# A two-layer encoder on one core: head and attention ordered as one graph by a list scheduler, with negated logits and the sink as a column of the logits

## The chip, the core and the metric

The kernel runs on one core of one Trainium2 chip. The metric is device time in microseconds: from the start to the end of one execution. TensorE (PE) multiplies matrices into PSUM, VectorE (DVE) and ScalarE (ACT) work on tiles in SBUF and PSUM, GpSimd (POOL) is nearly unused, SyncE (SP) and ScalarE issue DMAs. Each engine takes its instructions in the order of the program, and waits on semaphores for the others.

## The reference

Two request groups (512 and 256 tokens, 1024 features) pass through two layers with shared weights. Layer 0 mixes tokens by windowed attention, layer 1 by a short convolution; each is followed by an MLP and by a gated input embedding.

```python
def trunk(x, p, rel_bias, ...):
    band_bias, in_window = band_geometry(rel_bias)
    for i in range(DEPTH):                                  # DEPTH = 2
        h = rms_norm(x, norm_mix[i])
        if i % N_MIXERS == 0:
            x = x + window_attention(h, attn_w_qkv[j], attn_w_o[j], attn_sink[j], band_bias, in_window)
        else:
            x = x + short_conv(h, conv_w_in[j], conv_w[j], conv_w_out[j])
        h = rms_norm(x, norm_mlp[i])
        x = x + jnp.square(jax.nn.relu(h @ mlp_w_up[i])) @ mlp_w_down[i]
        gate = jax.nn.sigmoid(rms_norm(x, norm_ple[i]) @ ple_w_gate[i])
        x = x + (p[i] @ ple_w_proj[i]) * gate
    return rms_norm(x, final_norm)

# in window_attention, for each block of 128 queries (a block sees itself and its two neighbours):
logits = einsum(q, k) * scale + band_bias
logits = jnp.where(valid, logits, NEG_INF)
m = jnp.maximum(jnp.max(logits, axis=-1, keepdims=True), sink_logit)
pexp = jnp.exp(logits - m)
denom = jnp.sum(pexp, axis=-1, keepdims=True) + jnp.exp(sink_logit - m)
probs = pexp / denom                                        # then probs @ v, and @ w_o
```

There are 16 query heads and 4 key heads of 64 features; four query heads share a key head. All is fp32.

## The kernel before

Activations lie transposed, features on the 128 partitions and the 768 tokens of both groups in the free dimension. An fp32 product is made of three fp32r matmuls: each operand is split into a high part (a ScalarE copy) and a low part (VectorE subtracts the high part from the source), and high by high, high by low and low by high are added up in PSUM (`split`, `weight`, `group`). A product over 768 tokens is a matmul of 512 and one of 256 columns, three times for each of the eight blocks of features.

`mixer_attention` is the stage that the change rewrites. It comes first in the program; the MLPs, the gated embeddings and the convolution follow, and their code stays.

The head of the stage stands in the order that is written, on ScalarE, TensorE, VectorE and SyncE (`manual_schedule`). It loads the first input embedding `p`, its projection, `x` in eight blocks and the first weights; projects the embedding (`step`, stored to `pj` in DRAM); scales and splits `x` (`Norm.block`, tiles `xs_mix`), sums its squares, makes the row of relative-position biases (`bp`, `brow`) and the first keys' product.

Behind it nothing fixes the order by hand: the framework orders the instructions from where they stand in the code and from buffers and dependencies. There the row of biases is stored 32 times, shifted, to DRAM (`skew`); the reciprocal norms follow (`rstd`), keys (`keys`: two chunks of two key heads, copied to both halves of the partitions by DMA, tiles `khh` and `kll`), queries (`queries`: eight chunks of two heads, copied by DMA to tiles `q`) and values (`values`, tiles `vp` in PSUM and `vv`).

`attend(g)` then runs for the four key heads over six blocks of 128 tokens (four of the first group, two of the second). A block has two or three key blocks, so its scores are 256 or 384 columns wide. For each block:

- scores of four heads, two matmuls each, into PSUM tiles `S` (L690, L691);
- `tensor_tensor_reduce` on VectorE (L692) adds the bias, writes logits to `L` (two heads to a tile, five buffers) and takes the maximum with the sink to `mx`;
- `nm` negates the maximum (L705), `es` is the exponential of the sink less the maximum (L707, L708);
- ScalarE takes exponentials in place with a running sum `sm` (L712); `es` is added (L713) and the sum inverted (L714);
- each head's row is scaled, the first of four on ScalarE (`NA = 1`, L718), three on VectorE (L720);
- for each key block TensorE transposes four heads to `pt` (L725), ScalarE copies to `ph` (L733), VectorE makes the low part `pl` (L734), and two matmuls add to `O` (L735, L736; one PSUM bank);
- ScalarE copies the lower half of `O` to `ot` (L738), VectorE adds the halves into `heads` (L743).

`beside` hands queries, the second keys, part of the second embedding's projection and the first output projections to fixed blocks, behind which their code stands. `load_bias` reads shifted windows of `skew`: for key heads 0 and 1 through ScalarE's queue, for 2 and 3 through SyncE's. Output projections (`output_part`, tiles `aos`, `w_o0`, `w_o1`) add to `xa`; the last of them run after the stage, in matmuls of 384 columns (L128).

Of the kernel before, what the change touches and what calls it, by code (L numbers as in the profile page):

```python
# [31 lines left out]
NA = 1  # L32
# [14 lines left out]
def trunk_kernel(ctx: ExitStack, tc: tile.TileContext, a: dict, out: bass.AP):  # L47
# [10 lines left out]
    act.preload_act_table_set(EXP_LN)  # L58
# [10 lines left out]
    sink = const.tile([P, HEADS], F32, name="sink")  # L69
    ident = const.tile([P, P], F32, name="ident")  # L70
# [393 lines left out]

    def mixer_attention():
        s1, s2 = ExitStack(), ExitStack()
        psum = s2.enter_context(tc.tile_pool(name="psK", bufs=3, space=PSUM))
        nonlocal tmp
        ap = s1.enter_context(tc.tile_pool(name="attn", bufs=2))
# [6 lines left out]
        def pair(j, name, dt=F32):  # L476
            return main.tile([P, 2, T], dt, tag=f"x{j}", name=name)

        x = [pair(j, "x_in") for j in range(KB // 2)]

        def xin(m):
            return x[m // 2][:, m % 2, :]

        ET = mybir.EngineType
        order = {ET.Activation, ET.PE, ET.DVE, ET.SP}
        norm = Norm(0, "mix0", range(16, 32), 0)
        xs = norm.xs

        split_products = False

        def products(terms):

            if not split_products:
                ps = psum.tile([P, 1024], F32, tag="mm", name="mm")
                group(ps, terms)
                yield ps[:, :T], 0, T
                return
            o = 0
            for i, n in enumerate(SEQS):
                ps = psum.tile([P, 512], F32, tag=f"mm{i}", name="mm", bufs=BM)  # L500
                group(ps, [(wh, wl, xh[:, o : o + n], xl[:, o : o + n]) for wh, wl, xh, xl in terms], n)
                yield ps[:, :n], o, o + n
                o += n

        def step(l, m, w, part, tag, vector):

            if tag == "L":
                t = ap.tile([P, T], F32, tag="L", name="pjs", bufs=BL)
            else:
                t = big("pjs")  # L510
            for ps, o, e in products(terms_of(w, part, col=m % 4 * P)):
                if vector:
                    dve.tensor_copy(t[:, o:e], ps)
                else:
                    act.activation(t[:, o:e], ps, AF.Copy)
            nc.sync.dma_start(pj[l][m], t[:])

        with tc.manual_schedule(engines=order):
            w0 = wp.tile([P, CH], F32, name="wraw", bufs=3)
            p0 = []  # L520
            for k in range(2):
                c = slice(512 * k, 512 * k + 512)
                nc.sync.dma_start(w0[:, c], a["proj"][0, 0, :, c])
                t = big("p")
                nc.sync.dma_start(t[:], a["p"][0, :, k, :])
                p0.append(t)
            w1 = fetch(a["proj"][0, 1])
            nc.sync.dma_start(vec[:], a["vec"][:])
            for m in range(KB):
                nc.sync.dma_start(xin(m), a["x"][m])  # L530
            wk = fetch(a["w_k"][0])
            rb = ap.tile([32, HEADS], F32, name="rb", bufs=1)
            nc.sync.dma_start(rb[:], a["rel_bias"][:])
            oh = ap.tile([32, 512], F32, tag="bias", name="oh", bufs=4)
            nc.sync.dma_start(oh[:], a["onehot"][:])
            mk = ap.tile([HEADS, 512], F32, tag="bias", name="mk", bufs=4)
            nc.sync.dma_start(mk[:], a["mask"][:].broadcast_to([HEADS, 512]))
            nc.sync.dma_start(sink[:], a["sink"][:].broadcast_to([P, HEADS]))

            hi = wp.tile([P, CH], F32R, name="whi", bufs=2)  # L540
            lo = wp.tile([P, CH], F32R, name="wlo", bufs=2)
            part0 = [], []
            for k in range(2):
                c = slice(512 * k, 512 * k + 512)
                split(hi[:, c], lo[:, c], w0[:, c])
                ph, pl = slot(10 + k, "p0h"), slot(12 + k, "p0l")
                split(ph[:], pl[:], p0[k][:])
                part0[0].append(ph[:])
                part0[1].append(pl[:])
            w0 = blocks(hi[:], 2), blocks(lo[:], 2)  # L550
            w1 = weight(None, 2, raw=w1)
            for i in range(KB):
                step(0, i, (w0, w1)[i // 4], part0, "L", i % 2)
                norm.block(i, xin(i))
                if i == 3:
                    wk = weight(None, KB, raw=wk)
                    wq = [fetch(a["w_q"][0])]

            bp = psum.tile([P, 512], F32, tag="S", name="bp", bufs=2)
            pe.matmul(bp[:HEADS, :], lhsT=rb[:], rhs=oh[:], start=True, stop=True)  # L560
            brow = tmp.tile([HEADS, 512], F32, tag="t", name="brow")
            dve.tensor_tensor(brow[:], bp[:HEADS, :], mk[:], ALU.add)
            kps = list(products(terms_of(wk, xs)))
            wq[0] = weight(None, KB, raw=wq[0])
            ss = norm.sum_squares(psum)

        with s1:
            rawv = [fetch(a["w_v"][:, :T])]
            wq.append(fetch(a["w_q"][1]))

            skew = dram.tile([HEADS, (ROWS + 1) * SKEW], F32, name="skew")
            nc.sync.dma_start(
                skew[:, : ROWS * SKEW].rearrange("h (i m) -> h i m", i=ROWS),
                brow[:, None, :SKEW].broadcast_to([HEADS, ROWS, SKEW]),
            )
            rawv += [fetch(a["w_v"][:, o : min(o + T, 2 * CH)]) for o in (T, 2 * T)]
            r = norm.rstd(psum, ss=ss)


            def keys(c, kps):  # L580
                t = big("kt")
                for ps, o, e in kps:
                    dve.tensor_tensor(t[:, o:e], ps, r[:, o:e], ALU.mult)
                hi = big("kh", F32R)
                lo = big("kl", F32R)
                split(hi[:], lo[:], t[:])
                for j in range(2):
                    g = 2 * c + j
                    khh[g], kll[g] = slot(KHI[g], "khh"), slot(KLO[g], "kll")
                    for dst, part in ((khh[g], hi), (kll[g], lo)):  # L590
                        for i in range(2):
                            nc.sync.dma_start(
                                dst[64 * i : 64 * i + 64, :].bitcast(F32),
                                part[64 * j : 64 * j + 64, :].bitcast(F32),
                            )

            def queries(c):
                w = wq[0] if c == 0 else weight(a["w_q"][c], KB, raw=wq[1] if c == 1 else None)
                t = big("qt")
                for ps, o, e in products(terms_of(w, xs)):  # L600
                    dve.scalar_tensor_tensor(t[:, o:e], ps, HD**-0.5, r[:, o:e], ALU.mult, ALU.mult)
                hi = big("qh", F32R)
                lo = big("ql", F32R)
                split(hi[:], lo[:], t[:])
                for j in range(2):
                    h = 2 * c + j
                    qst[h] = slot(QS[h % 8], "q")
                    for i, part in enumerate((hi, lo)):
                        nc.sync.dma_start(
                            qst[h][64 * i : 64 * i + 64, :].bitcast(F32),  # L610
                            part[64 * j : 64 * j + 64, :].bitcast(F32),
                        )

            rc = ap.tile([P, T // P], F32, name="rc", bufs=1)
            rt = psum.tile([P, 512], F32, tag="S", name="rt", bufs=2)
            for n in range(T // P):
                pe.transpose(rt[:, n : n + 1], r[0:1, n * P : (n + 1) * P], ident[0:1, 0:1])
            dve.tensor_copy(rc[:], rt[:, : T // P])
            keys(0, kps)


            vv = ap.tile([P, T // P, KV, 2, HD], F32R, name="vv", bufs=1)
            wv = [], []
            for i, raw in enumerate(rawv):

                m = min(T, 2 * CH - i * T)
                hi, lo = slot((4, 8, 10)[i], "wvh"), slot((5, 9, 11)[i], "wvl")
                split(hi[:, :m], lo[:, :m], raw[:, :m])
                for parts, t in zip(wv, (hi, lo)):
                    parts += blocks(t[:, :m], m // 256)  # L630
# [14 lines left out]
            for i in range(2):  # L645
                queries(i)
# [991 lines left out]
```

## Time and profile before

| | before |
|---|---|
| median of 3 runs | 1666.8 us (1666.33 to 1667.81) |
| profiled execution, span from first to last instruction | 1665.8 us |
| mean granted TensorE clock over the span | 0.994 |
| busy: TensorE, VectorE, ScalarE | 1637.0, 1407.8, 912.1 us |
| DMA, mean over the span | 87 GB/s |
| first matmul | 5.81 us |
| first matmul of the stage behind attention | 276.99 us |

A profile row names the line of the code, the engine and operation, the tiles as output<-inputs, the shape and how often it ran; then the busy time and the mean duration of one in ns, and the idle time just before such instructions with what ended it. PEld are TensorE's weight loads, which overlap its matmuls. A busy TensorE may still be slow, since matmuls overlap: the distance from start to start says how fast it really goes.

### The profile page before, as it was taken

What the parts mean: (1) busy time and instruction counts of PE and PEld (TensorE: products, weight loads), DVE (VectorE), ACT (ScalarE), POOL (GpSimd) and SP (SyncE); (2) the same over time, 40 slices, a digit from 0 to 9 for tenths busy, and PEclk for the clock granted to TensorE, in tenths of its full rate; (3) what the DMA queues carried; (4) which work ended last, traced back from release to release, by engine and by line L of the source; (5) the groups of instructions that cost most, each with busy time, mean ns of one, the idle gap of its engine ahead of it and who ended that gap; (6) DMA issues with size and microseconds to landing.
All of it is one profiled execution on the core that took longest, in us unless ns stands there. A gap on an engine that the chain in (4) does not pass through costs nothing. (4 is left out here: it accounts for less than half of the span.)

```text
span 1665.8 us, 24155 instructions
## 1 busy us (share of the span) xinstructions
PE 1637.0 (98%) x9422; PEld 1587.7 (95%) x9422; DVE 1407.8 (85%) x2305; ACT 912.1 (55%) x1448; POOL 1.0 (0%) x12
## 2 busy tenths in 40 slices
PE   8999999999999999999999999999999999999996
PEld 7888878999999999999999999999999999999986
DVE  6489888999899889977878887759989989998776
ACT  6377756855555555544654434555545545554555
POOL 0000000000000000000000000000000000000000
PEclk9999999999999999999999999999999999999998
DMA  8735422212222222232321222211222222222222
GB/s 265 180 113 145 136 76 73 99 57 70 76 77 69 72 76 66 74 96 73 114 67 58 77 66 78 82 54 51 76 64 86 67 72 70 75 76 79 80 86 99
DMA packets 47843, 144.59 MB, mean 87 GB/s; under 512 B 6080, under 2 KB 10688, under 8 KB 47728
## 3 DMA queue, kind: packets, MB, share of 16 engines
q1 hardware_dynamic: 46448, 141.47, 26.8%
q10 hardware_dynamic: 1280, 1.57, 0.4%
q8 instruction: 74, 1.21, 0.3%
q14 instruction: 41, 0.34, 0.1%
HBM read 123.10 MB, written 10.48 MB: 80 GB/s over the span
## 5 line engine op out<-in xcount | busy, mean ns | idle before, releaser
L428 ACT ACTIVATE whi<-sum 128x1024 fp32r<-128x1024 f32 x66 | 70.1, 1062 | 257.1 <-PE a L460 214.4
L460 PE MATMUL a<-xs,whi 128*128 128x384 f32 x608 | 118.1, 335 | 0.7 <-DVE y L1135 0.7
L460 PEld LDWEIGHTS a<-xs,whi 128*128 128x128 f32 x608 | 106.5, 188 | 1.6 <-DVE y L1135 1.3
L460 PE MATMUL b<-t,zhi 128*128 128x384 f32 x528 | 107.4, 336 | 0.0
L460 PE MATMUL a<-t,whi 128*128 128x384 f32 x528 | 107.3, 336 | 0.0
L460 PE MATMUL a<-t,zhi 128*128 128x384 f32 x528 | 107.2, 336 | 0.0
L1171 DVE TENSOR_TENSOR x<-x,a 128x384 f32<-128x384 f32 x112 | 62.1, 554 | 53.1 <-PE a L460 53.0
L460 PE MATMUL a<-act,whi 128*128 128x384 f32 x448 | 95.8, 334 | 0.0
L460 PEld LDWEIGHTS a<-t,zhi 128*128 128x128 f32 x528 | 93.3, 188 | 0.0
L460 PEld LDWEIGHTS b<-t,zhi 128*128 128x128 f32 x528 | 93.2, 188 | 0.0
L460 PEld LDWEIGHTS a<-t,whi 128*128 128x128 f32 x528 | 93.2, 188 | 0.0
L428 ACT ACTIVATE zhi<-sum 128x1024 fp32r<-128x1024 f32 x66 | 69.8, 1057 | 37.2 <-DVE sum L404 31.4
L439 DVE TENSOR_TENSOR wlo<-wraw,whi 128x1024 fp32r<-128x1024 f32 x72 | 87.7, 1217 | 0.0
L428 ACT ACTIVATE whi<-wraw 128x1024 fp32r<-128x1024 f32 x72 | 75.6, 1050 | 19.3 <-issue 15.8
L137 PE MATMUL mm<-xs_mix,whi 128*128 128x512 f32 (+1 forms) x320 | 82.9, 344 | 0.0
L439 DVE TENSOR_TENSOR zlo<-sum,zhi 128x1024 fp32r<-128x1024 f32 x66 | 80.3, 1217 | 0.5 <-ACT zhi L428 0.5
L439 DVE TENSOR_TENSOR wlo<-sum,whi 128x1024 fp32r<-128x1024 f32 x66 | 80.4, 1218 | 0.0
L460 PEld LDWEIGHTS a<-act,whi 128*128 128x128 f32 x448 | 79.3, 188 | 0.0
L82 ACT ACTIVATE whi<-wraw 128x1024 fp32r<-128x1024 f32 (+2 forms) x49 | 49.9, 1020 | 39.2 <-PE mm L128 15.0
L460 PE MATMUL a<-xs,wlo 128*128 128x384 f32 x304 | 65.0, 334 | 0.0
L83 DVE TENSOR_TENSOR wlo<-wraw,whi 128x1024 fp32r<-128x1024 f32 (+2 forms) x49 | 57.6, 1176 | 5.7 <-ACT whi L82 5.7
L460 PE MATMUL b<-t,zlo 128*128 128x384 f32 x264 | 61.1, 336 | 0.8 <-DVE zlo L439 0.8
(286 smaller groups left out, 4491.5 us busy)
## 6 DMA issues: line engine op xcount, KB each, us to landing
wraw<-in_up SPq DMA_DIRECT2D x64, 512.0 KB, 3.4
wraw<-in_down SPq DMA_DIRECT2D x64, 512.0 KB, 3.4
wraw<-in_w_in SPq DMA_DIRECT2D x24, 512.0 KB, 3.4
wraw<-in_gate SPq DMA_DIRECT2D x16, 512.0 KB, 3.4
pj<-pjs SPq DMA_DIRECT2D x16, 384.0 KB, 2.8
wraw<-in_w_q SPq DMA_DIRECT2D x8, 512.0 KB, 4.5
wraw<-in_w_out SPq DMA_DIRECT2D x8, 512.0 KB, 3.5
x_in<-in_x SPq DMA_DIRECT2D x8, 384.0 KB, 7.1
```

The source lines that it names most:

```text
L82: first = act.activation(hi, src, AF.Copy)
L83: dve.tensor_tensor(lo, src, hi.bitcast(F32), ALU.subtract)
L137: pe.matmul(ps[:, o:e], lhsT=w, rhs=x[:, o:e], start=i == 0 and j == 0, stop=i == n - 1 and j == 2,)
L428: act.activation(hi[:], src, AF.Copy)
L439: dve.tensor_tensor(lo[:], src, hi[:].bitcast(F32), ALU.subtract)
L460: pe.matmul(ps, lhsT=a, rhs=b, start=start and i == 0, stop=i == len(terms) - 1, skip_group_check=True)
L1171: dve.tensor_tensor(t[:, o : o + H], t[:, o : o + H], f, op)
```

## The change

Everything in `mixer_attention` becomes an operation of a graph (`Plan.op`) with an engine, a cost from a small formula, what it runs `after`, and which buffers it uses. A buffer's next use waits for all users of the one before (`Plan.ring`). `Plan.order` walks over the engines in modelled time, takes on each the ready operation with the longest way to the end (operations of attention on TensorE get a bonus of 10 us), and the code is emitted in that order, with `manual_schedule` on all five engines. The product of two blocks is an operation for each block of features (three matmuls), so products of several PSUM tiles can alternate.

In the computation: queries are scaled by the negative of the old factor and the bias row is negated, so `S` and `L` hold negated logits and the reduce takes a minimum with the negated sink (`nsink`); the exponential runs with scale -1 and that minimum as its bias. Column 0 of each head in `L` holds the negated sink, copied there by POOL; the exponential runs over it too, so the sum holds the sink's share, and `nm`, `es`, its exponential and the addition go. `NA` becomes 2. All bias loads go through SyncE. At the start, six matmuls of ones run before the first product, with the bias row between them; its inputs come through ScalarE's queue, and the load of the activation table stands behind those.

```diff
-NA = 1
+NA = 2
+URGENT = 10.0
...
+    class Plan:
+        OWN = {"PE": 0.0, "ACT": 0.13, "DVE": 0.12, "POOL": 0.1, "SP": 0.0}
+        OTHER = {"PE": 0.22, "ACT": 0.15, "DVE": 0.14, "POOL": 0.3, "SP": 0.1}
...
+        def order(self):
...
+            for o in reversed(self.ops):
+                tail = o.tail if o.tail is not None else self.OTHER[o.engine]
+                o.reach = o.cost + max((n.reach + (tail if o in n.after else 0.0) for n in nexts[id(o)]), default=0.0)
...
+            while any(waiting.values()):
+                best = None
+                for e, os in waiting.items():
+                    if os:
+                        t = max(free[e], min(o.ready for o in os))
+                        o = max((o for o in os if o.ready <= t), key=lambda o: o.reach + o.bonus)
+                        if best is None or t < best[0]:
+                            best = t, o
+                t, o = best
+                waiting[o.engine].remove(o)
+                o.start = t
+                free[o.engine] = t + o.cost
+                if o.tail is not None:
+                    pipe = max(pipe, t + o.cost + 1.7) + o.tail
+                    o.landed = pipe + 0.3
...
+        def A(n):
+            return 0.095 + 0.00084 * n
+        def V(n):
+            return 0.067 + 0.00104 * n
+        MM = {512: 0.2275, 256: 0.12}
...
+        rb_in = dma(rb, lambda: (rb.t[:], a["rel_bias"][:]), 2048, queue="ACT")
+        oh_in = dma(oh, lambda: (oh.t[:], a["onehot"][:]), 65536, queue="ACT")
+        mk_in = dma(mk, lambda: (mk.t[:], a["mask"][:].broadcast_to([HEADS, 512])), 32768, queue="ACT")
+        table = op("ACT", 1.28, lambda: act.preload_act_table_set(EXP_LN), behind=[mk_in])
...
+        d0 = first(warm, "PE", 3 * 0.45, dummy(3), [wide], [ones512.key])
+        bps = first(bp, "PE", 1.0, ..., [rb_in, oh_in, d0], [rb.key, oh.key])
+            lambda: dve.scalar_tensor_tensor(brow.t[:HEADS, :512], bp.t[:HEADS, :], -1.0, mk.t[:], ALU.mult, ALU.subtract),
+        d1 = op("PE", 3 * 0.3, dummy(3), [bps], [warm.key, ones512.key])
...
-                                dve.tensor_tensor_reduce(
-                                    L[:, j, :w],
-                                    S[:, :w],
-                                    bias[hp][:, j, j0 : j0 + w],
-                                    1.0,
-                                    sink[:, h : h + 1],
-                                    ALU.add,
-                                    ALU.max,
-                                    accum_out=mx[:, 2 * hp + j : 2 * hp + j + 1],
-                                )
...
-                        dve.tensor_scalar(nm[:], mx[:], -1.0, None, ALU.mult)
-                        dve.tensor_tensor(es[:], sink[:, hs], mx[:], ALU.subtract)
-                        act.activation(es[:], es[:], AF.Exp)
...
-                            act.activation(Lh, Lh, AF.Exp, bias=nm[:, h : h + 1], accum_out=sm[:, h : h + 1])
-                        dve.tensor_tensor(sm[:], sm[:], es[:], ALU.add)
...
+                    sunk = first(L, "POOL", 0.2, lambda L=L, H_=H_: nc.gpsimd.tensor_copy(
+                        L.t[:, :, 0:1], nsink[:, H_ : H_ + 2].rearrange("p (a b) -> p a b", b=1)), [turned])
...
+                    dve.tensor_tensor_reduce(
+                        L.t[:, j, 1 : 1 + w], S.t[:, :w], bias[hp].t[:, j, j0 : j0 + w], 1.0,
+                        nsink[:, H_ : H_ + 1], ALU.add, ALU.min, accum_out=mn.t[:, h : h + 1],
+                    )
+                args = "DVE", 0.40 if nk == 2 else 0.53, reduced, [s, bias[hp].ready, sunk, turned]
...
+                    act.activation(L.t[:, j, : 1 + w], L.t[:, j, : 1 + w], AF.Exp, bias=mn.t[:, h : h + 1], scale=-1.0,
+                                   accum_out=sm.t[:, h : h + 1])
...
+                args = "DVE", V(256), joined, [o_, last]
...
+        load_bias(0)
+        unit(2, "n")
+        unit(3, "t")
+        group_of_heads(0)
+        load_bias(1)
+        second_keys()
+        second_projected()
...
+            with tc.manual_schedule(engines={ET.Activation, ET.PE, ET.DVE, ET.SP, ET.Pool}):
+                for o in plan.order():
+                    o.run()
```

More of the change, by code (lines that the diff above doesn't have):

```diff
@@ L489, in mixer_attention @@
[L489 to L513, printed above, removed]
-                else:
[L515 to L520, printed above, removed]
-            for k in range(2):
[L522 to L565, printed above, removed]
@@ new lines, in first, with start, bank @@
+        def first(box, engine, cost, run, after=(), uses=(), lands=None):
+            def start():
+                box.t = box.make()
+                run()
+            behind = [box.ahead.op] if box.ahead is not None else []
+            box.op = op(engine, cost, start, [box.free, *after], [box.key, *uses], behind, lands)
+            plan.opened[box.key] = box.op
+            return box.op
+        def bank(tag, name="mm"):
+            return new(tag, PB[tag], lambda: psum.tile([P, 512], F32, tag=tag, name=name, bufs=PB[tag]))
@@ new lines, in mixer_attention, with dummy, run @@
+        wk = fetched(a["w_k"][0])
+        sink_in = dma(None, lambda: (sink[:], a["sink"][:].broadcast_to([P, HEADS])), 8192)
+        for u, v in zip(DMAS := [got[0][0], w0.landed[0], got[1][0], w0.landed[1], w1.landed[0], vec_in, *x_in, wk.landed[0], sink_in], DMAS[1:]):
+            v.behind.append(u)
+        def dummy(n):
+            def run():
+                for _ in range(n):
+                    pe.matmul(warm.t[:], lhsT=ones[:], rhs=ones512.t[:, :512], start=True, stop=True)
+            return run
```

772 lines of the change are left out of this document (554 added, 218 removed).

## Prediction

> **What bounds the kernel now.** I read the page first, then the stages, then the matmuls of the stage that is rewritten.
>
> ```profile
> PE 1637.0 (98%) x9422; PEld 1587.7 (95%) x9422; DVE 1407.8 (85%) x2305; ACT 912.1 (55%) x1448; POOL 1.0 (0%) x12
> ```
>
> TensorE is busy nearly all the time, so only gaps and slow matmuls in front of it can be won back. By stages (us, then busy time and number of instructions of each engine, granted clock, DMA share, GB/s):
>
> ```profile
> core 0: us, PE busy (x) PEld busy (x) DVE busy (x) ACT busy (x) POOL busy (x), PEclk, DMA share, GB/s
> 0.00:5.80 5.80, 0.00 (x0) 0.00 (x0) 1.22 (x5) 2.76 (x3) 0.70 (x6) 1.00 0.67 193
> 5.80:12.40 6.60, 6.59 (x17) 4.70 (x18) 3.82 (x4) 3.88 (x5) 0.00 (x0) 1.00 1.03 397
> 12.40:71.00 58.60, 58.60 (x379) 52.13 (x379) 35.72 (x43) 28.77 (x39) 0.00 (x0) 1.00 0.82 229
> 71.00:81.00 10.00, 6.30 (x24) 5.27 (x23) 4.93 (x17) 4.86 (x12) 0.00 (x0) 0.66 0.61 140
> 81.00:200.00 119.00, 118.72 (x711) 102.16 (x711) 106.22 (x331) 87.83 (x233) 0.00 (x0) 1.00 0.45 129
> 200.00:220.00 20.00, 17.20 (x94) 13.24 (x93) 17.23 (x45) 13.55 (x31) 0.00 (x0) 1.00 0.47 138
> 220.00:277.00 57.00, 55.89 (x333) 47.86 (x331) 49.09 (x137) 37.98 (x93) 0.00 (x0) 1.00 0.15 45
> 277.00:1665.80 1388.80, 1373.73 (x7874) 1362.29 (x7874) 1189.55 (x1725) 732.49 (x1038) 0.33 (x6) 1.00 0.23 76
> ```
>
> The change rewrites what runs up to 277 us; the 1388.8 us behind it keep their code. A busy TensorE is not a full one, because matmuls overlap: what counts is the spacing of their starts, when nothing holds them.
>
> ```profile
> 61.93 0.28 PE L637 MATMUL vp<-wvh,xs_mix 128*128 128x256 f32 x1
> 62.05 0.28 PE L638 MATMUL vp<-wvl,xs_mix 128*128 128x256 f32 x1
> ...
> 263.94 0.39 PE L735 MATMUL O<-ph,vv 128*128 128x512 f32 x1
> 264.17 0.39 PE L137 MATMUL mm<-aos,wlo 128*128 128x512 f32 x1
> ...
> 81.65 0.34 PE L690 MATMUL S<-khh,q 128*128 128x384 f32 x1
> 81.82 0.34 PE L691 MATMUL S<-kll,q 128*128 128x384 f32 x1
> ...
> 241.57 1.04 PE L725 MATMUL pt<-ident,L 128*128 128x128 f32 x8
> 242.36 0.36 PE L137 MATMUL mm<-aos,whi 128*128 128x256 f32 x1
> ```
>
> So 0.12 us for 256 columns, 0.23 for 512, 0.17 for 384, and 0.79 for eight transposes, 0.10 each. How many there are up to 277 us says the same view asked for one tile at a time: projections, values, scores, transposes, probabilities times values.
>
> ```profile
> 0.00:277.00 277.00, 183.61 (x865) 137.50 (x865) 23.12 (x37) 7.02 (x12) 0.99 0.49 142
> ...
> 0.00:277.00 277.00, 17.33 (x144) 17.24 (x144) 2.90 (x6) 2.83 (x6) 0.99 0.49 142
> ...
> 0.00:277.00 277.00, 42.09 (x192) 33.15 (x192) 47.42 (x96) 0.99 0.49 142
> ...
> 0.00:277.00 277.00, 32.64 (x224) 25.75 (x224) 36.39 (x56) 30.80 (x56) 0.99 0.49 142
> ...
> 0.00:277.00 277.00, 41.90 (x112) 20.29 (x112) 19.98 (x48) 14.28 (x24) 0.99 0.49 142
> ```
>
> Of the 865, 864 are this stage's, half of 512 and half of 256 columns; of the 192 scores a third (the blocks with three key blocks) has 384. That makes 432 + 112 = 544 by 0.2335 = 127.0; 432 + 144 + 128 = 704 by 0.119 = 83.8; 64 by 0.174 = 11.1; 224 by 0.10 = 22.4 (third digits: means over such neighbours). With 1.7 for the few others (bias row, sums of squares, transposed norms) the work is 246 us. The stage takes 277: 5.8 pass before the first matmul and 25 are lost. Where, I read from the stages by a warm mean: 0.176 us for 512 and 256 columns in turn, some 0.16 for the mixture of attention (711 in 119 us, crumbs included, are 0.167). 17 matmuls in 6.6 us at 5.8 to 12.4 should take 3.0, so 3.6 go to cold matmuls (the clock column has no entry that early; the spacing shows it). 24 in 10 us at 71 to 81 should take 3.8: 6.2 lost. 94 in 20 us at 200 to 220 should take 15: 5.0 lost. 1.2 go at the seam to the next stage. The remaining 9.2 are crumbs.
>
> ```profile
> 74.01 0.46 SPq L609 DMA_DIRECT2D q<-ql  x1
> 75.82 0.55 PE L690 MATMUL S<-khh,q 128*128 128x256 f32 x1 [2.61 <-DMA q<-ql]
> ...
> 276.99 0.93 PE L128 MATMUL mm<-aos,whi 128*128 128x384 f32 x4 [1.00 <-ACT whi L82]
> ```
>
> At 75.82 the second pair of heads was waited for: TensorE stood behind a copy of queries with projections still undone, and came back at half clock (0.66 over the stretch). The other kind of wait, in the chain of waits between 80 and 276 us (total, times, longest):
>
> ```profile
> PEld O L735 <- ACT ph L733: 6.6, 23, 0.7
> ```
>
> 23 times probabilities times values stood too close behind the ScalarE copy that they need. Both are faults of order, not lack of work.
>
> **The change, part by part.** *Matmuls:* the same 864, 144, 192, 224 and 112 stand in the new program, plus six warming ones; work stays 246.
>
> *VectorE and ScalarE.*
>
> ```profile
> L720 DVE TENSOR_SCALAR L<-L,sm 128x256 f32<-128x256 f32 x48 | 14.2, 349 | 0.2
> ...
> L718 ACT ACTIVATE L<-L,sm 128x256 f32<-128x256 f32 x16 | 8.0, 503 | 5.2 <-DVE sm L714 5.0
> ...
> L705 DVE TENSOR_SCALAR nm<-mx 128x4 f32<-128x4 f32 x24 | 3.9, 162 | 0.1
> L713 DVE TENSOR_TENSOR sm<-sm,es 128x4 f32<-128x4 f32 x24 | 3.8, 159 | 2.5 <-ACT L L712 2.2
> L707 DVE TENSOR_TENSOR es<-sink,mx 128x4 f32<-128x4 f32 x24 | 3.7, 156 | 0.0
> ```
>
> Negated logits remove `nm`; the sink as column 0 of `L` removes `es`, its exponential and the addition: 3.9 + 3.8 + 3.7 = 11.4 us of VectorE, and for each block two short steps on the path from scores to transposes. NA = 2 moves 16 scalings of 349 ns and 8 longer ones to ScalarE: 7.7 us less there, 12.9 more here (16 by 503 ns and 8 somewhat longer). From 71 to 277 VectorE was busy 4.93 + 106.22 + 17.23 + 49.09 = 177.5; some 158 remain, ScalarE goes from 144 to about 153. Both fit into the 190 us left, VectorE with little room. I price this at zero by itself: TensorE covers it, and if VectorE were the bound the 19 us would count in full.
>
> *Order.* Interleaving projections three matmuls at a time and moving PV away from `ph` should remove most of the crumbs and the hole at 200 to 220. It can't remove all: 24 blocks share one `O` bank, and the plan charges 0.33 us for a `heads` addition:
>
> ```profile
> L743 DVE TENSOR_TENSOR heads<-O,ot 64x256 f32<-64x256 f32 x48 | 20.0, 416 | 6.2 <-ACT ot L738 5.3
> ```
>
> I keep 5 us of the 14.2, between 2 (a sixth) and 12 (nearly all).
>
> *The head of attention.* In the new order 62 us of matmul work stand before the first score, so it starts near 69 us instead of 72.47, and projections, not a bare wait, stand between the scores of the first and the second pair of heads. Against it: all bias loads go to SP, ten of them ahead of the keys' copies.
>
> ```profile
> 72.47 0.39 PE L690 MATMUL S<-khh,q 128*128 128x256 f32 x1 [1.08 <-DVE vv L643]
> ...
> 32.84 0.34 SPq L572 DMA_DIRECT2D skew<-brow  x1
> ...
> bias<-skew ACTq DMA_DIRECT2D x16, 96.0 KB, 4.5
> ...
> skew<-brow SPq DMA_DIRECT2D x1, 1022.0 KB, 12.5
> ```
>
> The skew store (KB, then us to landing) moves from 32.84 us to about 24, behind the sixth projection's store, and lands near 36.5; SP's queue then stands at the bias loads until it has. A load of 96 KB takes between 0.25 us (the 397 GB/s of the stretch at 5.8) and 1.2 (the skew's own pace, 12.5 for 1022 KB). Ten hold back the last part of the values' weights, two query weights and the keys until 39 to 48.5, and these land after them. The values need theirs on TensorE at 48, the scores their keys at 69: I charge 2 us, nearer to the fast end since 397 GB/s was measured on loads and the 12.5 on a store, and keep 0 to 5. ScalarE loses sixteen bias issues that waited for the skew.
>
> *The start.* The six warming matmuls and the bias row stand before the first projection on TensorE, and the row waits for its one-hot table, now loaded by ScalarE's queue.
>
> ```profile
> 3.98 0.63 ACT L82 ACTIVATE whi<-wraw 128x512 fp32r<-128x512 f32 x1 [1.97 <-DMA wraw<-in_proj]
> ```
>
> The first load landed just before 3.98. If the table lands then, the bias row (one or two matmuls) and three warming ones, 0.4 to 0.6 us each cold (17 took 6.6), end near 6.5. So the first projection starts at 6.5 us (5.8 to 7.5) instead of 5.8, and TensorE has worked before: I leave 1 us of the 3.6 cold (0 to 3.6). [...]
>
> *The seam.* The plan ends on some 14 us of output projections with VectorE and ScalarE nearly free, so the next weights are split in time: 1.2 us gone.
>
> **Sum.** 6.5 + 246 + 1 + 2 + 5 = 260.5 us instead of 277. With 1388.8 the span is 1649.3 against 1665.8; the runs' median, 1666.8, lies 1.0 above the span, so 1650.3: 16.5 faster. Lower end: 5.8 + 246 + 0 + 0 + 2 gives 1643.6. Upper end of the known terms: 7.5 + 246 + 3.6 + 5 + 12 gives 1663.9.
>
> **Rivals.** *VectorE's fixed order becomes the wait.* At 158 of 190 us busy, each late step holds what stands behind it, and a fixed order doesn't adapt: the 14.2 us of hole and crumbs come back in other places. Then 9.2 more, 1659.5. For: `heads` is underpriced in the plan, by 48 times 0.1 us; against: the stage before lost little at the same load.
>
> *The sink columns hold up each block.* 48 POOL copies now stand between a freed `L` and its first reduce; five `L` buffers serve two a block, so one of them is waited for.
>
> ```profile
> 1.00 0.29 POOL masks.py:199 TENSOR_SCALAR_AFFINE_SELECT ident<-ident 128x128 f32<-128x128 f32 x1
> ...
> L83 DVE TENSOR_TENSOR wlo<-wraw,whi 128x1024 fp32r<-128x1024 f32 x16 | 19.5, 1218 | 2.0 <-ACT whi L82 2.0
> ```
>
> A copy of two columns should take less than the 0.29 us row. But if each is held until a running weight split of 1.22 us ends, on the path of 24 blocks, it costs 29 us: 1679.6. It decides from 19.8 / 24 = 0.83 us a block, where the result is 0.2% above before. [...] Against: splits are few, and the copies can run a block ahead.
>
> *The order brings nothing.* If the lost 14.2 us are restarts of TensorE and not waits, and bias loads take away what the head gains, the time stays near 1666: within 0.2%, 3.3 us, which is about what a measurement of this kernel can tell from no change.
>
> **Chances.** Forecast (gain of 10 to 23 us) 0.70; VectorE's order 0.14; no change 0.06; sink columns or the like 0.10. The range, 1643 to 1662, takes in the first two and leaves out 0.16 to 0.2. Faster 0.84, same 0.06, slower 0.10.
>
> **What would show it.** The first matmul of the next stage (now at 276.99) near 260; no stretch of TensorE below clock 1 after 12 us; PV waits for `ph` under 3 us; first score near 69. Wrong, if VectorE waits for POOL before the reduces, if scores wait for keys or bias beyond 75 us, or if the 1388.8 us behind the stage move.

## The result, and the profile after

The changed kernel takes 1678.3 us (median of 4 runs, 1677.3 to 1679.7) beside 1667.2 us before in the same runs: 1.0067 of it, 95% interval 1.0053 to 1.0081. It is 11 us slower; 16.5 us faster was forecast. The profiled execution spans 1677.3 us.

The busy times of the profile after, then its stages (us, then busy time and number of instructions of each engine, granted clock, DMA share, GB/s):

```profile
PE 1641.3 (98%) x9428; PEld 1594.0 (95%) x9428; DVE 1394.3 (83%) x2215; ACT 919.9 (55%) x1454; POOL 13.5 (1%) x60
```

```profile
0.00:8.60 8.60, 4.90 (x9) 2.13 (x10) 4.42 (x9) 3.28 (x4) 0.70 (x6) 1.00 0.80 264
8.60:30.00 21.40, 21.22 (x120) 18.40 (x118) 17.59 (x23) 19.38 (x29) 1.33 (x2) 1.00 0.95 343
30.00:50.80 20.80, 20.72 (x121) 17.73 (x120) 13.14 (x18) 8.93 (x13) 2.15 (x4) 1.00 0.84 163
50.80:92.00 41.20, 31.29 (x173) 27.40 (x172) 10.79 (x20) 8.17 (x15) 0.00 (x0) 0.88 0.68 161
92.00:170.00 78.00, 77.89 (x497) 69.51 (x496) 63.88 (x178) 65.27 (x162) 4.55 (x20) 1.00 0.41 117
170.00:200.00 30.00, 24.45 (x125) 21.36 (x124) 14.24 (x41) 10.75 (x27) 0.74 (x4) 0.85 0.57 134
200.00:287.80 87.80, 86.49 (x522) 74.51 (x520) 80.26 (x208) 71.72 (x171) 3.69 (x19) 0.99 0.27 78
287.80:1677.30 1389.50, 1374.38 (x7874) 1362.95 (x7874) 1189.95 (x1725) 732.42 (x1039) 0.33 (x6) 1.00 0.23 76
```

Two stages stand out: 50.8 to 92 us and 170 to 200 us, where TensorE is idle for 9.9 and 5.6 us and has a clock of 0.88 and 0.85. Counted as in the prediction (distance of starts less the undisturbed distance of such matmuls), 15 us are lost in the first and 10 us in the second. From 92 to 170 us, in the middle of attention, 1.6 us are lost in all.

TensorE's instructions around the long waits (start, duration, operation; in brackets the idle time before it and what ended it):

```profile
50.81 0.28 PE L664 MATMUL mm<-xs_mix,wlo 128*128 128x256 f32 x1
53.41 0.39 PE L980 MATMUL vp<-wvh,xs_mix 128*128 128x256 f32 x1 [2.33 <-ACT wvh L691]
...
67.83 0.39 PE L664 MATMUL mm<-xs_mix,wlo 128*128 128x512 f32 x1
72.88 0.58 PE L980 MATMUL vp<-wvh,xs_mix 128*128 128x256 f32 x1 [4.66 <-DVE vv L998]
...
90.26 0.36 PE L1052 MATMUL S<-kk,q 128*128 128x256 f32 x1 [2.47 <-DMA q<-ql]
...
178.67 0.55 PE L1052 MATMUL S<-kk,q 128*128 128x256 f32 x1 [3.30 <-DMA bias<-skew]
...
196.47 0.36 PE L1052 MATMUL S<-kk,q 128*128 128x256 f32 x1 [2.24 <-DMA q<-ql]
...
287.83 0.58 PE L129 MATMUL mm<-aos,whi 128*128 128x384 f32 x2 [0.61 <-DVE xa L1163]
```

Five waits of 15.0 us together; most of the other 10 us lost are matmuls at a lower clock behind all but the one that ended at 90.26 us (the clock is 0.50 in the 2 us from 72.88 and from 178.67 us, 0.83 from 53.41, 0.91 from 196.47 and 1.00 from 90.26). A score reads no bias, so the wait that ended at 178.67 us is put down to the wrong transfer: the low copies of queries stood in the same queue just ahead of these bias loads, and the first of them, issued at 170.87 us, landed 7.7 us later, at 178.5 us, the bias loads behind it from 179.8 us on. The last row is the seam to the next stage: 287.83 us, where 260 was forecast and 276.99 measured before.

### The profile page after: what moved, and what is told of

Read it like the earlier page. It is cut to its first block, busy times and chain, and to the rows that moved or that the text cites. A ratio compares the mean times of both kernels' runs of the same rounds, so it can differ in the third digit from the quotient of the medians.

```text
span 1677.3 us, 24258 instructions
## 1 busy us (share of the span) xinstructions
PE 1641.3 (98%) x9428; PEld 1594.0 (95%) x9428; DVE 1394.3 (83%) x2215; ACT 919.9 (55%) x1454; POOL 13.5 (1%) x60
## 3 DMA queue, kind: packets, MB, share of 16 engines
q1 hardware_dynamic: 47600, 142.94, 27.3%
## 5 line engine op out<-in xcount | busy, mean ns | idle before, releaser
L664 PEld LDWEIGHTS mm<-xs_mix,whi 128*128 128x128 f32 x320 | 57.3, 200 | 6.0 <-ACT L L817 0.4
L1059 DVE CUSTOM_DVE_ANT_0 L<-S,bias,nsink 128x256 f32<-128x256 f32 (+1 forms) x96 | 48.1, 522 | 16.9 <-issue 10.7
L1069 ACT ACTIVATE L<-L,mn 128x257 f32<-128x257 f32 (+1 forms) x96 | 51.5, 539 | 19.3 <-DVE mn L1059 19.2
```

The costliest lines, as they stand in the source:

```text
L664: pe.matmul(ps.t[:, :n], lhsT=a_, rhs=b_, start=start and i == 0 and j == 0, stop=stop and i == len(ks) - 1 and j == 2,)
L1059: dve.tensor_tensor_reduce(L.t[:, j, 1 : 1 + w], S.t[:, :w], bias[hp].t[:, j, j0 : j0 + w], 1.0, nsink[:, H_ : H_ + 1], ALU.add, ALU.min, ...
L1069: act.activation(L.t[:, j, : 1 + w], L.t[:, j, : 1 + w], AF.Exp, bias=mn.t[:, h : h + 1], scale=-1.0, accum_out=sm.t[:, h : h + 1])
```

## Experiments

Two theories stood at the start. **A**: the bias loads on SP stand in front of the keys and the values' weights, only dearer than the 2 us charged. **B**: the plan's picture of the DMA queue is too rosy, so that the fixed orders ask for data before they land. A third, the sink columns, was a rival of the prediction. Ratios are to the kernel before, timed in the same runs, with 95% intervals.

**Bias loads behind the keys.**

```diff
+if g < 2:
+    b.ready[-1].behind.extend([raws[2].landed[0], *khh[0].ready, *kll[0].ready, *khh[1].ready, *kll[1].ready])
```

> The first sixteen bias loads may only be issued behind the keys' copies and the last part of the values' weights; the plan is otherwise as it was. Theory A (the bias loads in front of the keys' copies are the fault, as the prediction's step on the head of attention has it, only dearer than 2 us): the stall at 50.8 us (2.5 us and the cold matmuls after it, 4.8 lost between 50 and 60) goes and the later ones shrink with it: 5 to 12 us faster than the changed kernel, 1665 to 1672. Theory B (the plan prices the transfers too cheaply, so TensorE's order asks for data before the DMA queue can have delivered it, whatever stands first in the queue): the same bytes pass in another order, the stall near 68 us stays, and the gain is 1 to 3 us, 1674 to 1676.

Measured: 1678.4 us, 1.0066 (1.0051 to 1.0081); no change. The first copy of keys was issued at 46.59 us instead of 49.40, but the last part of the values' weights at 47.20 us instead of 47.11, since the new order put it behind that copy. The wait at 50.8 us shrank from 2.33 to 0.58 us, and the one near 68 us grew from 4.66 to 7.39:

```profile
51.85 0.39 PE L980 MATMUL vp<-wvh,xs_mix 128*128 128x256 f32 x1 [0.58 <-ACT wvh L691]
...
73.46 0.58 PE L980 MATMUL vp<-wvh,xs_mix 128*128 128x256 f32 x1 [7.39 <-DVE vv L998]
```

So theory A doesn't explain the loss: putting the bias loads behind only moved the wait. In the last run below ten bias loads still stand in front of the keys, SP takes 4.56 us to issue them, and most of the loss in the head is gone.

**The prices of transfers in the plan.** The price is a transfer's time in the queue (`slow` replaces the bytes divided by 400 KB/us). Shortened:

```diff
-lands = n / 400e3
+lands = n / 400e3 if slow is None else slow
...
+copies of keys and queries: slow=0.85
+skew store: slow=13.0
+weights, when len(plan.ops) >= 400: slow=P * 4 * n / 280e3
```

> Only the plan's prices of transfers change, to what the changed kernel's trace shows: 0.85 us instead of 0.49 for a copy of keys or queries, 13 instead of 10.5 for the skew store, 1.9 instead of 1.3 for 512 KB of weights behind the start. Theory B: the order then asks for the data when it is there; the stalls near 51, 68 and 87 us with their cold matmuls (15 us) go, and most of those near 175 and 194 (8 us): 1656 to 1664, faster than before the change. Theory A: biases are still in front of much, a small gain of up to 5 us, 1672 or more.

Measured: 1660.3 us, 0.9955 (0.9939 to 0.9972), 18 us faster than the changed kernel by a change of three numbers in the plan. Next, its two halves.

> Of the three prices only that of the copies of keys and queries is made true (0.85 us instead of 0.49); the skew store and the weights stay too cheap. Theory B, copies above all: the stalls near 68, 87, 175 and 194 us go, the one near 51 (third part of the values' weights behind the skew) stays: 1661 to 1666. If the skew's or the weights' price matters more: 1668 or more.

> The other half of the price experiment: the skew store at 13 us and the weights behind the start at 1.9 us, the copies at the changed kernel's 0.49. All three together gave 18 us, the copies alone 12. If the parts add up: 6 us faster than the changed kernel, 1670 to 1674. If either half alone gives the plan enough slack in the head: 10 us or more, 1664 to 1668.

Measured: copies alone 1666.0 us, 0.9994 (0.9985 to 1.0004); the other two alone 1671.4 us, 1.0017 (1.0007 to 1.0028). 12.4 and 6.9 us less than the changed kernel: together 19, about the 18 of all three.

**More lead instead of true prices.**

```diff
-tail = o.tail if o.tail is not None else self.OTHER[o.engine]
+tail = o.tail + 8.0 if o.tail is not None else self.OTHER[o.engine]
```

> Prices as in the changed kernel; only in the longest way to the end does a transfer count 8 us more than its bytes, so that TensorE makes what has to be copied earlier. Theory B: another way to give the copies their lead; the stalls near 68, 87, 175 and 194 us go or shrink, the one near 50 stays: 10 to 15 us faster than the changed kernel, 1662 to 1667. Theory A: no change of the first stalls, within 3 us of 1677.

Measured: 1658.4 us, 0.9944 (0.9929 to 0.9959), more than expected; the stall near 50 us went too. So no true price is needed. The low copies of queries still land 6.3 us after their issue (median) with this lead and 6.0 us with true prices, as against 6.3 us in the changed kernel: both remedies change when the copies are made and asked for, and leave the queue as slow as it was. With true prices and 4 us of lead together:

> All three true prices, and 4 us more for each transfer in the longest way to the end. Theory B: the waits for queries that each of the two alone left near 165, 180 and 207 us (2 to 4 us with their cold matmuls) go: 1653 to 1657. If the two are one and the same remedy and what is left is bandwidth: 1657 to 1660.

Measured: 1658.5 us, 0.9947 (0.9933 to 0.9962): the two don't add up, and 2.7 us are still lost between 70 and 80 us and 3.7 between 160 and 170 us, by the distances of starts, at scores that wait for queries.

**Sink columns three times.**

```diff
-nc.gpsimd.tensor_copy(L.t[:, :, 0:1], ...)
+for _ in range(3):
+    nc.gpsimd.tensor_copy(L.t[:, :, 0:1], ...)
```

> Each of the 48 POOL copies of the sink into column 0 is made three times. If the sink columns hold up each block, by a lock or by a wait of the reduces, 96 more copies of some 0.25 us stand in the path of 24 blocks, two to four in each: 12 to 24 us slower than the changed kernel, 1689 to 1701. If they run a block ahead beside the other engines, as the other theories have it: within 1.5 us of 1677.

Measured: 1679.7 us, 1.0073 (1.0058 to 1.0088), within 1.5 us of the changed kernel. POOL's copies, of the changed kernel and of this one, as far as the stage goes:

```profile
L1044 POOL COPY L<-nsink 128x2 f32<-128x2 f32 x48 | 12.5, 267 | 249.2 <-PE pt L1095 175.6 <-DVE nsink L771 26.7 <-ACT L L1069 23.1
```

```profile
L1046 POOL COPY L<-nsink 128x2 f32<-128x2 f32 x144 | 34.4, 250 | 228.1 <-PE pt L1098 164.8 <-DVE nsink L771 26.6 <-ACT L L1072 14.9
```

A copy takes 0.25 to 0.27 us on average, and 22 us more of them cost nothing that the intervals can tell: POOL is the one that waits, for `L` to be free, and no instruction of the changed kernel waits for one of its copies. So the rival of the sink columns is dead. Single copies are held up, though. The copies of the changed kernel (number, shortest, median and longest in ns), then the first of them and VectorE's addition beside it:

```profile
L1044 POOL COPY L<-nsink x48: 182/187/1411, 28.0 to 262.7; 128x2 f32<-128x2 f32 x48
```

```profile
28.02 0.77 POOL L1044 COPY L<-nsink 128x2 f32<-128x2 f32 x1 [26.72 <-DVE nsink L771]
```

```profile
27.79 0.95 DVE L848 TENSOR_TENSOR acc<-acc,sq 128x768 f32<-128x768 f32 x1
```

Six of the 48 take 0.43 to 1.41 us, and each of the six ends 0.05 us behind the end of a VectorE instruction with two inputs in SBUF that ran beside it. So single copies were held as the rival supposed; what holds them, no run here shows. It costs nothing here because the copies run ahead of the reduces (the first of each start at 28.0 and 84.4 us).

**The arithmetic alone, in the old order,** with two scalings of a block on ScalarE and then with one.

```diff
 kernel before:
+nc.gpsimd.tensor_copy(L[:, :, 0:1], nsink[...])
-nm, es, exponential of es, sm + es
+act.activation(Lh, Lh, AF.Exp, bias=mx[...], scale=-1.0, accum_out=sm[...])
-NA = 1
+NA = 2
```

> The kernel before with the new arithmetic alone: negated logits, the sink as column 0 of the logits (POOL copies), two scalings on ScalarE; its own order, its own bias loads. If VectorE's 24 us less and the two short steps less a block are hidden by TensorE (the prediction's zero): 1664 to 1669, no change. If they stand on the path: each block some 0.3 us shorter, 5 to 9 us faster. If the POOL copies hold up the blocks: slower.

> As the run of the arithmetic alone, which took 8 us more than the kernel before, but with one scaling of a block on ScalarE and three on VectorE, as before. If the second ScalarE scaling costs the 8 us (transposes waited 4.8 us for ScalarE's scaled logits there): 1664 to 1669, the time before. If the column of the sink, its POOL copies or the longer exponential cost it: 1672 or more.

Measured: 1675.7 us, 1.0050 (1.0035 to 1.0065), and with `NA = 1` 1679.4 us, 1.0074 (1.0059 to 1.0089). The first is slower, the third of its cases; the second lies above 1672, the case that charges the sink column, its POOL copies or the longer exponential. The traces don't bear that reason out: the 64 exponentials of 257 columns are busy for 31.9 us (32.0 in the changed kernel), those of 256 columns for 31.8 us before, and in neither run is a wait put down to POOL's copies (one reduce of the second stands for 2.0 us, with nothing named that it waits for). In the first, transposes wait for ScalarE's scaled logits (4.8 us, before 1.6):

```profile
PEld pt L722 <- ACT L L715: 4.8, 13, 1.1
```

But with `NA = 1` that wait shrinks to 2.0 us and the time grows. The framework orders these two kernels anew from their instructions: between 78 and 100 us they run 28 and 40 matmuls of projections, the kernel before 59, and their scores wait 4.6 and 4.4 us for copies of queries, before 2.9. So these runs compare orders too. What the arithmetic costs by itself in a fixed order stays open; what they show is that the old order is no safe place for it.

**One scaling on ScalarE under the plan** (`NA = 1`; compared with the run with the new start, below).

> As the run with prices, lead and the new start, but with one scaling of a block on ScalarE; the plan is made anew for it. If the plan hides the second ScalarE scaling and VectorE has the room (the prediction's zero): within 3 us of 1657. If ScalarE's second scaling costs here too: 3 to 8 us faster. If VectorE, with 12.9 us more to do, becomes the wait: 3 to 10 us slower.

Measured: 1661.3 us, 0.9966 (0.9953 to 0.9979), against 1657.2 us, 0.9942 (0.9925 to 0.9958): some 4 us slower, the third of the cases, the intervals overlapping a little. TensorE's weight loads for probabilities times values wait 3.8 us (13 times) for VectorE's low part `pl` there, against 0.8 us (3 times) with two scalings on ScalarE. VectorE has 6.9 us more to do (the 12.9 us of the expectation is what the prediction put on ScalarE). So under a plan without the large waits the relief of VectorE seems to be worth some 4 us, where the prediction priced it at zero; the interval doesn't quite settle it.

**The start.**

```diff
-three warming matmuls, bias row, three warming matmuls, then the first projection
+d0 = first(warm, "PE", 12 * 0.43, dummy(12), [wide], [ones512.key])
+bps.behind.append(<second matmul operation of the first projection>)
```

> As the run with all prices and 4 us of lead, and at the start twelve warming matmuls in a row, with the bias row behind the first projection instead of in front of it. The first products have all they need by 7.1 us and by then TensorE has worked without a break: first product at 6.2 to 7 us instead of 8.6, warm at once: 1.5 to 2.5 us faster than without. If the first products wait for something else (the splits of the first weights), no change.

Measured: 1657.2 us, 0.9942 (0.9925 to 0.9958), 1.3 us less than without by the medians, not resolved by the intervals; in the trace the scores' waits are still there and the first product moves from 8.41 to 6.89 us. In the changed kernel, where it starts at 8.59 us:

```profile
7.73 1.05 PE L755 MATMUL warm<-warm,ones 128*128 128x512 f32 x2
8.59 0.63 PE L664 MATMUL mm<-p0h,whi 128*128 128x512 f32 x1
9.01 0.63 PE L664 MATMUL mm<-p0l,whi 128*128 128x512 f32 x1
```

0.42 us from start to start is a cold matmul of 512 columns here. With the twelve in a row (the kernel with the held loads, below, has the same start; the first row is a stage, the number behind its busy time that of its matmuls):

```profile
1.76:5.34 3.58, 3.58 (x8) 1.00 0.94 286
```

```profile
4.92 1.56 PE L758 MATMUL warm<-warm,ones 128*128 128x512 f32 x5
6.32 0.39 PE L667 MATMUL mm<-p0h,whi 128*128 128x512 f32 x1
```

Eight take 3.58 us, 0.45 each; the first product and those behind it are warm (0.23 us from start to start). In the run with the new start alone the same twelve stay cold for longer: the last three take 1.28 us there, from 5.77 us on, and 0.86 us here, from 5.62 us on.

**Large loads held back.** Where a chunk of queries is copied, ScalarE's high part is ready before VectorE's low part. In the gap the plan's SP issues whatever is ready. Of the changed kernel (SP's queue: issue, its duration, transfer):

```profile
168.54 1.12 SPq L617 DMA_DIRECT2D q<-qh  x2
169.75 0.54 SPq L617 DMA_DIRECT2D wraw<-in_w_o  x1
170.38 0.41 SPq L617 DMA_DIRECT2D xa<-in_x  x1
170.87 1.11 SPq L617 DMA_DIRECT2D q<-ql  x2
```

```diff
+HELD = {12: (2, 3), 16: (4, 5), 19: (8, 9), 20: (10, 11)}    # large load: heads whose copies go first
+for h in HELD.get(raw.key[1], ()):
+    raw.landed[0].behind.extend(qst[h].ready)
+if m in (1, 3):
+    xa[m].ready[0].behind.extend([*qst[8].ready, *qst[9].ready])
```

First with prices, lead and the new start, and with 8 us of lead:

> As the run with prices, lead and the new start, but six large loads (512 KB of weights or 384 KB each) that the plan put between the high and the low copies of a chunk of queries may only be issued behind the low copies. In that run such a load landed 3.8 to 4.4 us behind the copies ahead of it instead of 1.3, and the low copies behind it at 77, 164 and 176 us. If these large loads hold the low copies back: the scores' waits at 75.8, 162 and 175 us (1.3, 2.1 and 0.7 us, with cold matmuls behind the second) go: 3 to 5 us faster, 1652 to 1655. If the low copies are late by themselves, no change.

> As the run with the held loads, with 8 us of lead instead of 4. If what is left are waits for copies: another 0 to 2 us, 1651 to 1654. If more lead pushes other work off its time, the crumbs between 90 and 260 us grow by 1 to 3 us: 1654 to 1657.

Measured: 1654.1 us, 0.9926 (0.9909 to 0.9942), and with 8 us of lead 1655.2 us, 0.9931 (0.9916 to 0.9946), the same within the intervals. The first is 3.1 us below the run without the held loads, where the intervals overlap, and is the fastest kernel of all: 24 us below the changed kernel and 12.6 below the kernel before. Its stages:

```profile
30.00:90.00 60.00, 60.00 (x388) 54.51 (x387) 33.73 (x66) 26.66 (x53) 0.87 (x4) 1.00 0.75 179
90.00:170.00 80.00, 79.84 (x497) 70.27 (x497) 64.01 (x176) 62.87 (x154) 4.97 (x22) 1.00 0.53 148
170.00:200.00 30.00, 30.00 (x187) 26.79 (x186) 29.11 (x76) 27.45 (x65) 2.09 (x8) 1.00 0.25 72
```

```profile
260.11 0.58 PE L129 MATMUL mm<-aos,whi 128*128 128x384 f32 x2 [0.60 <-DVE xa L1169]
```

TensorE never stops between 30 and 90 us, and from 170 to 200 us it makes 187 matmuls instead of 125. The next stage begins at 260.1 us (this profiled execution is its fastest, 1.7 us below its median). Then the held loads alone, in the changed kernel with its own prices, lead and start:

> The changed kernel with its own prices, and only the six large loads held behind the low copies of queries. If large loads between the high and the low copies make the second group of stalls (175 and 194 us; 9.9 us lost between 170 and 200 us, cold matmuls included), most of that goes and the first group stays: 6 to 10 us faster than the changed kernel, 1668 to 1672. If the copies are late because the projections come too late, and not because of what stands between them: 1675 to 1679.

Measured: 1665.8 us, 0.9992 (0.9983 to 1.0001), 12.5 us less than the changed kernel, more than expected: the wait at 90 us was of this kind as well (a load of `in_p` stood between its copies) and is gone, and the one at 50.8 us shrank from 2.33 to 0.26 us in the new order. Transfers of the stage (number, KB each, median us from issue to landing), of the changed kernel and of this run:

```profile
q<-qh SPq DMA_DIRECT2D x16, 192.0 KB, 3.1
q<-ql SPq DMA_DIRECT2D x16, 192.0 KB, 6.3
```

```profile
q<-qh SPq DMA_DIRECT2D x16, 192.0 KB, 3.0
q<-ql SPq DMA_DIRECT2D x16, 192.0 KB, 3.1
```

High and low copies are alike, mostly issued 1 to 2.3 us apart; with large loads between many of them the low ones take twice as long, 6.3 us instead of 3.1.

**And the split of the second embedding behind the values.** What is left of the first group is the wait near 68 us. ScalarE's instructions there, of the changed kernel:

```profile
61.56 0.47 ACT L995 ACTIVATE vv<-vp,rc 128x256 fp32r<-128x256 f32 x1 [5.13 <-PE vp L982]
70.59 0.84 ACT L1180 ACTIVATE p<-wraw 128x768 fp32r<-128x768 f32 x1 [8.56 <-DMA wraw<-in_p]
71.34 0.46 ACT L995 ACTIVATE vv<-vp,rc 128x256 fp32r<-128x256 f32 x1
```

ScalarE waits 8.56 us for an input that nobody needs yet; behind it in its fixed order stands the copy of values that frees TensorE's PSUM bank.

```diff
+h.behind.append(vready[T // P - 1][0])
```

> As the run with only the large loads held, and besides ScalarE splits the second embedding's input (which landed at 70.4 us, 13 us behind the plan's time) only behind its last copy of values. Prices are the changed kernel's own. If ScalarE's fixed order, standing at this split while TensorE waited for a free PSUM bank of the values, makes the stall at 66.8 us (5.7 us and cold matmuls; 7.8 lost between 60 and 80): 6 to 9 us faster than without, 1657 to 1660. If the values would then wait for something else: within 2 us of 1665.8.

Measured: 1657.5 us, 0.9945 (0.9929 to 0.9962), 8.3 us less than with the held loads alone. The next stage begins at 264.63 us:

```profile
264.63 0.59 PE L129 MATMUL mm<-aos,whi 128*128 128x384 f32 x2 [0.60 <-DVE xa L1168]
```

Two repairs by hand, of six loads and one split, with the plan's own wrong prices, take back 21 of the 28 us between forecast and result.

## Why the prediction was wrong

*Work.* The changed kernel makes 9428 matmuls in all, six more than before, as forecast. In the fastest kernel the first product starts at 6.3 us and the stage ends at 260.1 us; beside 246 us of work that leaves 7.8 us, where the forecast kept 8 and ended at 260.5. That the two ends agree so closely is partly luck, since that kernel has a start, prices and holds that the forecast didn't have.

*Order.* The mechanism was right. The waits of probabilities times values for `ph`, 6.6 us in 23 before, are in the changed kernel (total, times, longest)

```profile
PEld O L1110 <- ACT ph L1104: 0.4, 1, 0.4
```

and the stage from 92 to 170 us loses 1.6 us. Of the 5 us kept for crumbs in the whole stage that would do. But the term knew only waits between engines. The 10 us between 170 and 200 us come from the same list, by what it puts on SP's queue: the step "Interleaving ... should remove most of the crumbs and the hole at 200 to 220" overlooked that the list orders transfers too.

*The head of attention* is the step that failed first: 2 us charged, 0 to 5 kept, 15 measured. Its parts, in the changed kernel (of the ten bias loads the first three):

```profile
27.21 0.42 SPq L617 DMA_DIRECT2D skew<-brow  x1
...
42.46 1.26 SPq L617 DMA_DIRECT2D bias<-skew  x3
```

```profile
skew<-brow SPq DMA_DIRECT2D x1, 1022.0 KB, 15.2
```

The skew store was issued at 27.21 us (forecast about 24) and took 15.2 us (12.5 before), so the queue stood until 42.4 us and not 36.5. The bias loads themselves were as cheap as priced: SP issued ten in 4.55 us, 0.46 us each where 0.25 to 1.2 was reckoned, and moving them changed nothing in the time. What the step left out is what comes behind: it asked what ten loads delay, and took for granted that each engine would meet its data once these had passed. The lists are fixed by modelled times; each transfer that is late beyond them holds an in-order queue, SP's (4.5 us behind the skew store), then ScalarE's (8.56 us at the split of `in_p`), then TensorE (4.66 us at 72.88), and four of its five long stops were paid again in cold matmuls (clock 0.50 to 0.91 in the 2 us behind them). First score at 69 us was forecast. The changed kernel's scores, and those of the kernel with prices, lead, start and held loads (number, shortest, median and longest in ns, first and last start in us, of those up to 100 us):

```profile
L1052 PE MATMUL S<-kk,q x8: 278/340/423, 83.0 to 96.1; 128*128 128x256 f32 x4, 128*128 128x384 f32 x4
```

```profile
L1056 PE MATMUL S<-kk,q x16: 278/308/422, 69.5 to 99.2; 128*128 128x256 f32 x8, 128*128 128x384 f32 x8
```

A late first score costs nothing by itself: with 8 us of lead and the held loads it starts at 78.8 us, and that kernel takes 1655.2 us. What costs is TensorE standing still before it.

*The start.* 6.5 us and 1 us cold, the author's estimate, were forecast; 8.59 us and cold to about 10 (0.42 us from start to start) measured, 2 us more. The row of biases waits for its inputs until 5.35 us and its matmuls (1.03 us each, 0.59 before) and the three behind it (1.65 us together) are cold. With twelve in a row the first product starts at 6.9 us, and at 6.3 us with the held loads, both times warm (its busy time is 0.39 us, in the changed kernel 0.63).

*VectorE and ScalarE.* Priced at zero. None of the changed kernel's long waits is for a reduce, an exponential or a scaling, so the 28 us didn't go here; VectorE is 13.5 us less busy over the whole kernel, not 19. What its relief is worth is between nothing and the some 4 us of the run with `NA = 1`; no run isolates it in a fixed order.

*Seam and what is behind.* The wait for the split weights is gone as forecast, but one of 0.61 us for `xa` stands in its place; behind it 1389.5 us instead of 1388.8.

Together: 2 more at the start, 13 in the head, 10 from 170 to 200 us and 3 to 4 in crumbs (5 were kept, 8.5 counted outside these stages, the seam among them) make 28 to 29, against 27.3 between 260.5 and 287.8 us; the counted distances are good to about 1 us.

*Rivals.* "A fixed order doesn't adapt" was the first rival's reason, and it is what happened. It was tied to VectorE, and priced with what the order might fail to gain, 9.2 us, instead of with what it might newly lose. The range missed the result because no case had the order itself lose more than it removes. The price of the sink columns, 1679.6 us, lies next to the measured 1678.3 by accident: it charges a hold of 1.22 us in each of 24 blocks, which no run shows; six copies of 48 were held, 0.43 to 1.41 us long, and nothing waits for them. Of the signs named, the waits of PV for `ph` came true; the clock (0.88 and 0.85), the first score (83 us) and the next stage (287.8 us) didn't.

## What to carry to other kernels

The fixed orders that this list scheduler wrote were as good as its picture of the transfers; true prices, more lead and held loads, each alone, took back 18, 20 and 12.5 us. Read from the trace of before what each kind takes in a full queue, and ask of each in-order queue what stands behind its next late item. Give copies that TensorE will wait for several us of lead, issue the parts of one operand back to back, and let nothing large in between. When such a change disappoints, sort the long waits by what ended them before touching the schedule's rules: here six loads and one split were worth 21 us.

## What the runs showed of the hardware

Copies from SBUF to SBUF kept the DMA engines as busy as loads at little more than half the rate, 230 against 407 GB/s. Three stages of the changed kernel: inputs at the start, a stretch of almost nothing but the skew store, and one of copies of keys (a store of `pj` at its end).

```profile
12.00:16.80 4.80, 4.80 (x26) 4.01 (x25) 3.27 (x4) 3.63 (x6) 0.00 (x0) 1.00 1.04 407
30.00:39.00 9.00, 9.00 (x51) 7.78 (x50) 6.34 (x9) 5.45 (x9) 1.78 (x2) 1.00 0.92 96
150.90:156.20 5.30, 5.30 (x34) 4.66 (x33) 5.09 (x13) 4.92 (x14) 0.37 (x2) 1.00 1.02 230
```

The engines are busy in all three (1.04, 0.92 and 1.02); they move 407, 96 and 230 GB/s. By division, a copy of 192 KB takes 0.85 us at 230 GB/s and would take 0.49 at the plan's 400. The loads fill 128 partitions, a copy covers 64, and the store reads 16: the rates fall in the same order, but no run here varies that alone, so why the copies and the store are slower stays open.
